# Spreading per-head rows over the partitions: 64-row matmuls or DMAs from a DRAM tile

## Chip, cores and metric

The kernel runs on one core of one Trainium2 chip. The metric is the device time of one execution in microseconds; 2156.14 us is the median of three runs before the change.

## The reference

A trunk of two layers over 512 tokens of width 1024, in float32. Each layer is a half-step SwiGLU FFN, a token mixer, and another half-step FFN; every sublayer has an RMSNorm before and after it and is modulated by shift, scale and gate vectors made from a conditioning vector. Layer 0's mixer is an mLSTM (4 heads), layer 1's a Mamba-2 SSD (32 heads in 4 groups). What matters here are the scalars per head and token:

```python
# mLSTM, per head; the kernel takes all 512 tokens as one chunk
b = cumsum(lf); log_d = b[t] - b[s] + ig[s]      # s <= t
m_t = max over s of log_d
s = (q @ k.T) * exp(log_d - m_t)
h = (s @ v) / max(|sum(s)|, exp(-m_t))
# Mamba-2, per head, chunks of 128 tokens
a = cumsum(dt * A)
y = ((C @ B.T) * exp(a[t] - a[s]) * dt[s]) @ x + exp(a[t]) * (C @ state)
```

In both, a matrix with the source token in the partitions needs a row over the target tokens (the running maximum, or `a`) in every partition.

## The kernel before

Features or tokens lie in the 128 partitions, 512 columns to a tile. All large products are made of float32r heads and rests: `mm3` (L175) issues three matmuls, head by head (L177), head by rest (L178) and rest by head (L179, by the order of the operands). Weights arrive in units of 128 x 1024 through `unit` (L150): a DMA on SP's queue into one of four `raw` buffers (L153), a copy to the head on ACT (L165), and the rest on DVE (L166), into one of three `wh` and `wl` buffers each. `proj` (L468) runs eight blocks of `mm3` over a unit into one of four `mm` PSUM banks; other PSUM work takes one of four `aux` banks (`ps_aux`).

SBUF working tiles come from 52 slots of 128 x 512 (`slot`, L98), handed on in the order in which they are freed. The program is written as a list of steps, in which `weave` (L1038) and `spread` (L1046) put projections between the steps of the mixers' heads; a scheduler then fixes the order of each engine's queue at build time, by readiness and the order of writing. At run time each queue is in order.

mLSTM: `rows` (L673) makes running sums and maxima for the heads as rows of [32, 512] tiles, and `split_rows` (L625) turns such a tile into a float32r [64, 512] tile, heads over rests (ACT L628, DVE L629). `pick(h)` (L632) is a stationary operand of 64 rows that selects row h and its rest; one matmul then spreads that row over 128 partitions. `head` (L713) does so for the negated maximum `nM` (L716), reads the result from PSUM on ACT (Relu L720, Exp L721), and for the denominator's `nm` (L748), with an exponential on ACT behind it (L750, `em`).

Mamba-2: `rows` (L803) makes `a` by a scan (L814) and splits it (L816). `ssm(g)` (L901) takes the eight heads of a group, two to a `yp` bank. For each head one matmul spreads `a` (L956); ACT makes the decay in `w` (four Relu L959, one Exp L961); DVE multiplies by the masked scores (L963); four matmuls L965 per head (the trace counts each as two) apply it. For each pair of heads a matmul with the operand `pair` (L948) puts one row into 64 partitions and the other into the other 64, for 384 columns (L970); ACT takes its exponential (`ea`, L972); DVE multiplies the state's share by it (L976) and adds it (L979).

The step of a Mamba pair, whose matmuls the change is about:

```python
                    pa = ps_aux()
                    matmul(pa, pick(h), self.ar[0:64], start=True, stop=True)
                    w = slot(name="w")
                    for c in range(4):
                        act(w[:, c * P:(c + 1) * P], pa[:, c * P:(c + 1) * P], AF.Relu, scale=-1.0,
                            bias=cols[:, P + c * 32 + h:P + c * 32 + h + 1])
```

The trunk weaves `ml.head(0..3)` with the value and output-gate projections (L1126 to L1129, with `pump`, which adds the modulation's steps L194 to L199), `mb.ssm(0..2)` with projections of the next group (L1151 to L1156), and spreads `mb.ssm(3)` over projections of `z` and the output product of groups 0 to 2 (L1157 to L1161).

Of the kernel before, what the change touches and what calls it, by code (L numbers as in the profile page):

```python
# [9 lines left out]
F32 = mybir.dt.float32  # L10
# [5 lines left out]
P = 128  # L16
T = 512
# [12 lines left out]
# log1p(e) = e * (c0 + e * (c1 + ...)) on [0, 1], relative error below 1e-8  # L30
# [26 lines left out]
def trunk(ctx: ExitStack, tc: tile.TileContext, i: dict, out: bass.AP):  # L57
# [21 lines left out]
    class Slots:  # L79
        """Tiles of one size, each place with a tag of its own; a place is handed on in the order of the frees."""  # L80
# [30 lines left out]
    # ------------------------------------------------------------ constants  # L111
# [29 lines left out]
    sel_f = const.tile([64, 32], F32, name="sel_f")  # L141
    nc.gpsimd.tensor_tensor(sel_f, ident[0:64, 0:32], ident[0:64, 32:64], ALU.add)
    sel = const.tile([64, 32], F32R, name="sel")
    nc.gpsimd.tensor_copy(sel, sel_f)
# [4 lines left out]
    # ------------------------------------------------------------ weights  # L149
    def unit(src, n=1024, hold=False, soon=True):  # L150
        """A block of weights [128, n] as its float32r head and the exact rest, in tiles of `step` columns."""
        raw = rawp.tile([P, 1024], F32, tag="raw", name="raw")
        nc.sync.dma_start(raw[:, :n], src)  # L153
        if hold:
            step = T
            his = [slot(F32R, "wh") for _ in range(-(-n // T))]
            los = [slot(F32R, "wl") for _ in range(-(-n // T))]
        else:
            step = 1024
            his = [whp.tile([P, 1024], F32R, tag="wh", name="wh")]  # L160
            los = [wlp.tile([P, 1024], F32R, tag="wl", name="wl")]
        with tc.high_priority() if soon else nullcontext():
            for q, (hi, lo) in enumerate(zip(his, los)):
                a, b = q * step, min(q * step + step, n)
                act(hi[:, :b - a], raw[:, a:b], AF.Copy)  # L165
                tt(lo[:, :b - a], raw[:, a:b], hi[:, :b - a].bitcast(F32), ALU.subtract)  # L166

        def part(a, w):
            q = a // step
            c = slice(a - q * step, a - q * step + w)  # L170
            return his[q][:, c], los[q][:, c]
        part.tiles = his + los if hold else []
        return part

    def mm3(ps, stat, mov, first, last):  # L175
        """ps += stat.T @ mov for operands given as (head, rest)."""
        matmul(ps, stat[0], mov[0], start=first, stop=False)  # L177
        matmul(ps, stat[0], mov[1], start=False, stop=False)  # L178
        matmul(ps, stat[1], mov[0], start=False, stop=last)  # L179
# [5 lines left out]
    # ------------------------------------------------------------ adaLN  # L185
# [3 lines left out]
    def ada_kind(l, s, kind):  # L189
# [43 lines left out]
        def gate_rows(parts):  # L233
            """The gate times the post norm's weight, the same row in every partition."""
            G[l, s] = []
            for c in range(2):
                rows = []
                for name in ("gate_b", "norm_post"):
                    rows.append(slot(name="row"))
                    nc.sync.dma_start(rows[-1], i[name][l * 3 + s:l * 3 + s + 1, c * T:(c + 1) * T].to_broadcast([P, T]))  # L240
                ps = ps_aux()
                for q, t in enumerate(parts[c]):
                    matmul(ps, ones_r, t, start=q == 0, stop=q == 1)
                g = slot(name="grow")
                tt(g, ps, rows[0], ALU.add)
                stt(g, g, 0.5 if s != 1 else 1.0, rows[1], ALU.mult, ALU.mult)
                G[l, s].append(g)
                free(*rows, *parts[c])
                done_ps(ps)
# [17 lines left out]
    # ------------------------------------------------------------ norms  # L267
    def newton(out, r0, v):
        """out = r0 * (1.5 + v * r0 * r0), v = -0.5 * (mean + eps)."""
# [4 lines left out]
    def ones_mm(ps, src):  # L274
        """ps = the sum over the partitions of src, on every partition."""
# [6 lines left out]
    def rstat(src, scale):  # L282
        """rsqrt(scale * (sum over partitions of src) + eps) on every partition, in src's place."""
# [10 lines left out]
    def rcol(ss, more=None):  # L294
        """rsqrt((ss + more) / D + eps), [128, 1]"""
# [23 lines left out]
    class Pre:  # L319
        """x's modulated norm, tokens in partitions, to hm, features in partitions."""  # L320
# [44 lines left out]
    def dot(raws, v):  # L365
        """The sum over kc of block kc of the raws times v[:, kc]."""
# [8 lines left out]
    def dot_end(acc, col):  # L375
        """mod0[:, col] = the sum over the partitions."""
# [6 lines left out]
    class Start(Pre):  # L383
        """The first sublayer's input: scaled first, with the shift put in later."""
# [49 lines left out]
    class Post:  # L434
        """Adds the sublayer's normed, gated output to x, a block of tokens at a time."""
# [31 lines left out]
    # ------------------------------------------------------------ projections  # L467
    def proj(ps, wt, hm, sl, m=P):  # L468
        """ps[:m, sl] = (1024 x m weights).T @ hm; wt: a unit of [128, 8 * m]."""
# [4 lines left out]
    def out_main(y, units, acts, first, last):  # L474
        """y[t] += acts[k][:, t].T @ weights, 2 k a unit"""
# [10 lines left out]
    def out_tail(ys, groups, first, done):  # L486
        """The same, block of tokens by block; groups: a list of (units, acts) for each of ys."""
# [15 lines left out]
    def out_proj(units, acts, tail, post):  # L503
        """units: [2, n / 2, 128, 1024]; the second half's last `tail` units go block by block of tokens."""
# [18 lines left out]
    class Ffn:  # L523
# [7 lines left out]
        def weights_kept(self, f):  # L531
            """The weights of f, loaded to slots that keep them."""
# [18 lines left out]
        def early(self, k, hm, ps):  # L551
            """Block k's share in the first columns, without the shift; ps: a pair for each f."""
# [9 lines left out]
        def late(self, f, q, kept):  # L562
            """The shift's share of columns f."""
# [49 lines left out]
    # ------------------------------------------------------------ rows: log1p(exp(-|x|))  # L613
# [11 lines left out]
    def split_rows(src):  # L625
        """[32, T] rows as a float32r [64, T]: heads over rests."""
        t = slot(F32R, "rows")
        act(t[0:32], src, AF.Copy)  # L628
        tt(t[32:64], src, t[0:32].bitcast(F32), ALU.subtract)  # L629
        return t  # L630

    def pick(h):  # L632
        """Stationary operand that spreads row h (and its rest) over the partitions."""
        return sel[:, h:h + 1].to_broadcast([64, P])

    # ------------------------------------------------------------ mLSTM
    class Mlstm:
# [35 lines left out]
        def rows(self):  # L673
# [14 lines left out]
            self.nM = split_rows(m)  # L688
            self.nm = split_rows(b)
# [23 lines left out]
        def head(self, h):  # L713
            k, q, vt = self.k[h], self.q[h], self.vt[h]
            pm = ps_aux()
            matmul(pm, pick(h), self.nM[0:64], start=True, stop=True)  # L716
# [8 lines left out]
            done_ps(pm)  # L725
# [21 lines left out]
            pn = ps_aux()  # L747
            matmul(pn, pick(h), self.nm[0:64], start=True, stop=True)  # L748
            em = slot(name="em")
            act(em, pn, AF.Exp)  # L750
            done_ps(pn)
# [37 lines left out]
    # ------------------------------------------------------------ Mamba-2  # L789
    class Mamba:  # L790
# [12 lines left out]
        def rows(self):  # L803
# [12 lines left out]
            self.ar = split_rows(a)  # L816
# [18 lines left out]
            done_ps(ps)  # L835
            free(self.dtr, ta, tw)
# [15 lines left out]
        def conv(self, ch, hm, ps=None):  # L852
            """silu(conv) of the 128 channels of block ch, [channel, token]."""
# [47 lines left out]
        def ssm(self, g):  # L901
# [20 lines left out]
            for c in range(4):  # L922
# [6 lines left out]
                if c < 3:  # L929
# [9 lines left out]
                    else:  # L939
# [6 lines left out]
            tp = slot(F32R, "pair")  # L946
            pair = tp[0:64]
            nc.vector.tensor_copy(pair.rearrange("p (h e) -> p h e", e=64),  # L948
                                  sel_f[:, g * 8:g * 8 + 8].unsqueeze(2).to_broadcast([64, 8, 64]))
            for j in range(4):  # L950
                yp = ps_aux()
                for e in range(2):
                    hh = 2 * j + e
                    h = g * 8 + hh
                    pa = ps_aux()
                    matmul(pa, pick(h), self.ar[0:64], start=True, stop=True)  # L956
                    w = slot(name="w")
                    for c in range(4):
                        act(w[:, c * P:(c + 1) * P], pa[:, c * P:(c + 1) * P], AF.Relu, scale=-1.0,  # L959
                            bias=cols[:, P + c * 32 + h:P + c * 32 + h + 1])  # L960
                    act(w, w, AF.Exp, scale=-1.0)  # L961
                    done_ps(pa)
# [6 lines left out]
                pa, yi = ps_aux(), ps_aux()  # L969
                matmul(pa[:, P:], pair[:, j * P:(j + 1) * P], self.ar[0:64, P:], start=True, stop=True)  # L970
                ea = slot(name="ea")
                act(ea[:, P:], pa[:, P:], AF.Exp)  # L972
# [7 lines left out]
                done_ps(pa, yi, yp)  # L980
                free(ea)
                yield
            free(gs, Cf, tp, *xdt, *state[1:])
# [18 lines left out]
        def wout(self, *gs):  # L1002
            """Adds the share of the groups gs to yacc."""
# [34 lines left out]
    def weave(main, *others):  # L1038
        """Traces main's steps with the others' spread between them."""
# [6 lines left out]
    def spread(main, n, rest, m):  # L1046
        """Traces main's n steps with m of rest's spread evenly between them."""
# [6 lines left out]
    # ------------------------------------------------------------ the trunk  # L1054
# [77 lines left out]
    free(ml.nM, ml.nm)  # L1132
# [29 lines left out]
    free(mb.ar, mb.cols)  # L1162
# [8 lines left out]
def _layout(inputs):  # L1171
# [5 lines left out]
    def stat(w, m=P):  # L1177
        """[K, M] -> [M / m, 128, (K / 128) * m]: blocks of m columns, contiguous per partition."""
# [6 lines left out]
    def mov(w):  # L1185
        """[K, 1024] -> [2, K / 256, 128, 2 * 512]: blocks of 256 rows and 512 columns."""
# [6 lines left out]
    def cols(a):  # L1193
        """[..., n * 128] -> [128, ... * n]"""
        return c(a.reshape(-1, P).T)
# [60 lines left out]
```

## Time and profile before

| | |
|---|---|
| median of three runs | 2156.14 us (2155.45 to 2156.46) |
| profiled execution, first to last instruction | 2154.5 us |
| PE busy | 2129.8 us (99%), 10742 matmuls |
| DVE, ACT, POOL busy | 1259.7, 862.0, 11.0 us |
| granted TensorE clock, mean | 0.998 |
| DMA | 272.84 MB, mean 127 GB/s |

Of the profiled execution the page gives the span alone; the median of the runs is 1.6 us longer than it. Durations of matmuls in the trace overlap, since they are pipelined: how much of PE's time a matmul takes is read from the starts of its neighbours. The mLSTM heads lie at about 459 to 600 us, the Mamba heads at about 1429 to 1720 us.

### The profile page before, as it was taken

The page shows a single profiled execution, that of the slowest core. Times are in us where ns is not written, and L with a number is a line of the kernel's source. Part 1 is how long each engine was busy: PE and PEld are TensorE (multiplying, and loading weights), DVE is VectorE, ACT ScalarE, POOL GpSimd, SP SyncE. Part 2 cuts the span into 40 slices and gives each one's busy share as a digit, 9 for nine tenths or more (in the row PEclk, how much of TensorE's full clock was granted, in tenths as well). Part 3 has the DMA queues.
Part 4 walks back from the last instruction along what each step waited for, and adds up shares of the span by engine and source line. Part 5 has one row for each costly group of instructions (what it writes and reads, how often), then busy time and mean ns, then how long its engine had stood idle before and what let it go on. Part 6 is the DMA issues. An engine that isn't in the chain of part 4 may idle for free.

```text
span 2154.5 us, 27065 instructions
## 1 busy us (share of the span) xinstructions
PE 2129.8 (99%) x10742; PEld 1769.0 (82%) x10742; DVE 1259.7 (58%) x1942; ACT 862.0 (40%) x1420; POOL 11.0 (1%) x35
## 2 busy tenths in 40 slices
PE   7999999999999999999999999999999999999998
PEld 5888888988789888889888888987777789888887
DVE  8976524758885775237574323877887756333323
ACT  5433323535562333236333223646555645222221
POOL 0000000000000000000000000000000000000000
PEclk9999999999999999999999999999999999999999
DMA  7666534143435776343574333221221132233331
GB/s 273 188 198 222 188 98 132 50 134 121 127 108 180 241 228 196 96 144 101 176 231 128 98 98 120 79 62 57 78 60 59 59 118 79 83 96 96 98 107 59
DMA packets 81535, 272.84 MB, mean 127 GB/s; under 512 B 10241, under 2 KB 10369, under 8 KB 81409
## 3 DMA queue, kind: packets, MB, share of 16 engines
q1 hardware_dynamic: 81408, 271.12, 39.7%
q8 instruction: 84, 1.38, 0.3%
q14 instruction: 43, 0.34, 0.1%
HBM read 268.99 MB, written 2.10 MB: 126 GB/s over the span
## 4 chain that ended last, share of the span: by engine, by line
PE 95%; DVE 2%; DMA 1%; ACT 1%; issue 0%; SPq 0%; DVEq 0%; ACTq 0%
PE mm L177 25%; PE mm L179 25%; PE mm L178 25%; PE aux L177 4%; PE aux L179 4%; PE aux L178 4%; PE aux L965 1%; PE aux L336 1%; PE aux L974 1%; PE aux L743 1%; PE aux L956 1%; PE aux L934 0%; DMA a<-in_ada 0%; PE aux L729 0%; DMA raw<-in_ada_w 0%
## 5 line engine op out<-in xcount | busy, mean ns | idle before, releaser
L177 PE MATMUL mm<-hm,wh 128*128 128x512 f32 (+1 forms) x2128 | 773.7, 366 | 2.7 <-ACT hm L350 1.3
L179 PE MATMUL mm<-hm,wl 128*128 128x512 f32 (+1 forms) x2128 | 770.6, 363 | 0.0
L178 PE MATMUL mm<-hm,wh 128*128 128x512 f32 (+1 forms) x2128 | 770.0, 363 | 0.0
L165 ACT ACTIVATE wh<-raw 128x1024 fp32r<-128x1024 f32 (+1 forms) x402 | 372.0, 941 | 764.3 <-PE mm L178 279.2
L166 DVE TENSOR_TENSOR wl<-raw,wh 128x1024 fp32r<-128x1024 f32 (+1 forms) x402 | 427.5, 1075 | 415.4 <-ACT wh L165 407.6
L177 PEld LDWEIGHTS mm<-hm,wh 128*128 128x128 f32 x2128 | 399.2, 188 | 69.5 <-issue 6.9
L179 PEld LDWEIGHTS mm<-hm,wl 128*128 128x128 f32 x2128 | 400.3, 188 | 63.0 <-issue 3.3
L178 PEld LDWEIGHTS mm<-hm,wh 128*128 128x128 f32 x2128 | 400.3, 188 | 62.5 <-issue 3.6
L199 DVE SCALAR_TENSOR_TENSOR acc<-raw,csil,acc 128x1024 f32<-128x1024 f32 x112 | 143.7, 1283 | 146.5 <-DMA raw<-in_ada_w 145.7
L589 DVE TENSOR_TENSOR s<-s,mm 128x512 f32<-128x512 f32 (+1 forms) x97 | 59.9, 618 | 134.0 <-PE mm L179 133.9
L177 PE MATMUL mm<-wh,gh 128*128 128x512 f32 x352 | 137.5, 391 | 0.0
L179 PE MATMUL mm<-wh,gl 128*128 128x512 f32 x352 | 137.0, 389 | 0.0
L178 PE MATMUL mm<-wl,gh 128*128 128x512 f32 x352 | 137.0, 389 | 0.0
L177 PE MATMUL aux<-wh,gh 128*128 128x512 f32 x352 | 136.9, 389 | 0.0
L178 PE MATMUL aux<-wl,gh 128*128 128x512 f32 x352 | 136.9, 389 | 0.0
L179 PE MATMUL aux<-wh,gl 128*128 128x512 f32 x352 | 136.9, 389 | 0.0
L182 ACT ACTIVATE gh<-s 128x512 fp32r<-128x512 f32 (+1 forms) x100 | 57.9, 580 | 130.3 <-DVE s L589 121.6
L179 PEld LDWEIGHTS mm<-wh,gl 128*128 128x128 f32 x352 | 66.1, 188 | 13.8
L179 PEld LDWEIGHTS aux<-wh,gl 128*128 128x128 f32 x352 | 66.1, 188 | 13.8
L178 PEld LDWEIGHTS aux<-wl,gh 128*128 128x128 f32 x352 | 66.1, 188 | 13.7
L177 PEld LDWEIGHTS aux<-wh,gh 128*128 128x128 f32 x352 | 66.1, 188 | 13.7
L178 PEld LDWEIGHTS mm<-wl,gh 128*128 128x128 f32 x352 | 66.1, 188 | 13.5
(276 smaller groups left out, 2188.7 us busy)
## 6 DMA issues: line engine op xcount, KB each, us to landing
raw<-in_w SPq DMA_DIRECT2D x258, 512.0 KB, 3.7
raw<-in_ada_w SPq DMA_DIRECT2D x128, 512.0 KB, 4.2
raw<-in_mb_wx SPq DMA_DIRECT2D x24, 512.0 KB, 3.6
a<-in_ada SPq DMA_DIRECT2D x32, 256.0 KB, 5.4
raw<-in_mb_wz SPq DMA_DIRECT2D x16, 512.0 KB, 3.6
raw<-in_mb_wout SPq DMA_DIRECT2D x16, 512.0 KB, 3.6
raw<-in_ml_wkq SPq DMA_DIRECT2D x8, 512.0 KB, 3.9
raw<-in_ml_wv SPq DMA_DIRECT2D x8, 512.0 KB, 3.6
```

Source lines behind the costliest of these rows:

```text
L165: act(hi[:, :b - a], raw[:, a:b], AF.Copy)
L166: tt(lo[:, :b - a], raw[:, a:b], hi[:, :b - a].bitcast(F32), ALU.subtract)
L177: matmul(ps, stat[0], mov[0], start=first, stop=False)
L178: matmul(ps, stat[0], mov[1], start=False, stop=False)
L179: matmul(ps, stat[1], mov[0], start=False, stop=last)
L182: act(dst_h, src, AF.Copy)
L199: stt(st["acc"], raw, csil[:, kc:kc + 1], st["acc"], ALU.mult, ALU.add)
L336: nc.tensor.transpose(self.pt[d // 2][:, o:o + P], scr[:, d * P:(d + 1) * P], ident)
L589: tt(s[:, a:b], s[:, a:b], p[1][:, a:b], ALU.mult)
L743: matmul(num[j][:, c * P:], vt[c // 2][:, o:o + P], st[c][:, c * P:], start=c == 0, stop=c == 3)
L956: matmul(pa, pick(h), self.ar[0:64], start=True, stop=True)
L965: matmul(yp[e * 64:(e + 1) * 64, c * P:(c + 1) * P], xdt[c][:, hh * 64:(hh + 1) * 64], w[:, c * P:(c + 1) * P], start=True, stop=True)
```

## The change

The rows are written to a DRAM tile once, and each head's row is loaded from there into all partitions. `split_rows`, `pick`, `sel`, `sel_f` and `pair` go, and with them the matmuls L716, L748, L956 and L970 and the PSUM banks they wrote. The exponentials of L750 and L972 are taken once on the rows, ahead of the write. ACT reads the spread rows from SBUF. Comments and docstrings go too, so that line numbers stay close.

```diff
+    class Rows:
+        def __init__(self, name, src):
+            n = src.shape[0]
+            self.got = {}
+            self.ap = tc.dram_tile([n, T], F32, name=name)
+            nc.sync.dma_start(self.ap, src)
+
+        def load(self, key):
+            if key in self.got:
+                return
+            t = slot(name="bc")
+            w = P // len(key)
+            for q, h in enumerate(key):
+                nc.sync.dma_start(t[q * w:(q + 1) * w], self.ap[h:h + 1, :].to_broadcast([w, T]))
+            self.got[key] = t
+
+        def take(self, key):
+            self.load(key)
+            return self.got.pop(key)
...
-            self.nM = split_rows(m)
-            self.nm = split_rows(b)
+            self.nM = Rows("ml_nM", m[0:4])
+            act(b, b, AF.Exp)
+            self.em = Rows("ml_em", b[0:4])
...
-            pm = ps_aux()
-            matmul(pm, pick(h), self.nM[0:64], start=True, stop=True)
+            pm = self.nM.take((h,))
...
-            done_ps(pm)
+            free(pm)
+            em = self.em.take((h,))
+            if h < 3:
+                self.nM.load((h + 1,))
...
-            pn = ps_aux()
-            matmul(pn, pick(h), self.nm[0:64], start=True, stop=True)
-            em = slot(name="em")
-            act(em, pn, AF.Exp)
-            done_ps(pn)
...
-            self.ar = split_rows(a)
+            self.ar = Rows("mb_a", a)
...
+            act(a, a, AF.Exp)
+            self.ea = Rows("mb_ea", a)
...
-            tp = slot(F32R, "pair")
-            pair = tp[0:64]
-            nc.vector.tensor_copy(pair.rearrange("p (h e) -> p h e", e=64),
-                                  sel_f[:, g * 8:g * 8 + 8].unsqueeze(2).to_broadcast([64, 8, 64]))
...
-                    pa = ps_aux()
-                    matmul(pa, pick(h), self.ar[0:64], start=True, stop=True)
+                    pa = self.ar.take((h,))
+                    if e == 0:
+                        self.ar.load((h + 1,))
+                        ea = self.ea.take((h, h + 1))
+                    elif h < 31:
+                        self.ar.load((h + 1,))
...
+                    free(pa)
                     act(w, w, AF.Exp, scale=-1.0)
-                    done_ps(pa)
...
-                pa, yi = ps_aux(), ps_aux()
-                matmul(pa[:, P:], pair[:, j * P:(j + 1) * P], self.ar[0:64, P:], start=True, stop=True)
-                ea = slot(name="ea")
-                act(ea[:, P:], pa[:, P:], AF.Exp)
+                yi = ps_aux()
```

## Rows read from the trace of the kernel before

**Rows 1.** The page, chain that ended last: shares of the span by engine.

```profile
PE 95%; DVE 2%; DMA 1%; ACT 1%; issue 0%; SPq 0%; DVEq 0%; ACTq 0%
```

**Rows 2.** Busy time by stretch: us, engines' busy time, PEclk, DMA share, GB/s.

```profile
0.00:80.00 80.00, 65.08 (x301) 52.92 (x302) 68.96 (x225) 44.20 (x70) 3.96 (x16) 1.00 0.66 225
...
1462.00:1530.00 68.00, 68.00 (x326) 49.47 (x325) 53.03 (x80) 42.11 (x87) 0.00 (x0) 1.00 0.18 56
...
1660.00:1720.00 60.00, 60.00 (x285) 44.04 (x284) 43.80 (x66) 35.04 (x69) 0.00 (x0) 1.00 0.19 54
```

**Rows 3.** PE in order of time around one L956: start, us, instruction.

```profile
1462.41 0.39 PE L178 MATMUL mm<-hm,wh 128*128 128x512 f32 x1
1462.64 0.39 PE L179 MATMUL mm<-hm,wl 128*128 128x512 f32 x1
1462.95 0.50 PE L956 MATMUL aux<-rows,sel 64*128 64x512 f32 x1
1463.38 0.50 PE L177 MATMUL mm<-hm,wh 128*128 128x512 f32 x1
1463.72 0.40 PE L178 MATMUL mm<-hm,wh 128*128 128x512 f32 x1
```

**Rows 4.** PE in order of time around one L970.

```profile
1478.72 0.40 PE L179 MATMUL mm<-hm,wl 128*128 128x512 f32 x1
1479.05 0.44 PE L970 MATMUL aux<-rows,pair 64*128 64x384 f32 x1
1479.42 0.50 PE L177 MATMUL mm<-hm,wh 128*128 128x512 f32 x1
1479.75 0.39 PE L178 MATMUL mm<-hm,wh 128*128 128x512 f32 x1
```

**Rows 5.** PE in order of time around two L956 in a row.

```profile
1639.80 0.40 PE L178 MATMUL mm<-hm,wh 128*128 128x512 f32 x1
1640.13 0.72 PE L956 MATMUL aux<-rows,sel 64*128 64x512 f32 x2
1640.78 0.50 PE L179 MATMUL mm<-hm,wl 128*128 128x512 f32 x1
1641.12 0.40 PE L177 MATMUL mm<-hm,wh 128*128 128x512 f32 x1
```

**Rows 6.** The four lines' matmuls: ns min/median/max, first and last start in us.

```profile
L956 PE MATMUL aux<-rows,sel x32: 387/497/502, 1463.0 to 1698.4; 64*128 64x512 f32 x32
...
L970 PE MATMUL aux<-rows,pair x16: 328/442/443, 1470.6 to 1701.0; 64*128 64x384 f32 x16
...
L716 PE MATMUL aux<-rows,sel x4: 497/497/498, 458.9 to 553.4; 64*128 64x512 f32 x4
...
L748 PE MATMUL aux<-rows,sel x4: 497/497/497, 478.4 to 573.5; 64*128 64x512 f32 x4
```

**Rows 7.** DMA issues: count, KB each, median us to landing.

```profile
row<-in_gate_b SPq DMA_DIRECT2D x12, 256.0 KB, 4.2
...
out_x<-x SPq DMA_DIRECT2D x8, 256.0 KB, 2.1
```

**Rows 8.** The tile `row`: its loads (a broadcast row of 512) on SP's queue.

```profile
L240 SPq DMA_DIRECT2D row<-in_gate_b x12: 327/328/425, 79.9 to 1100.8; - x12
...
DMA to landing us min/median/max: 3.4/4.6/6.3
```

**Rows 9.** Line L628, ACT: ns min/median/max, first and last start in us.

```profile
L628 ACT ACTIVATE rows<-fg x1: 630/630/630, 431.0 to 431.0; 32x512 fp32r<-32x512 f32 x1
...
L628 ACT ACTIVATE rows<-a x1: 632/632/632, 1403.1 to 1403.1; 32x512 fp32r<-32x512 f32 x1
```

**Rows 10.** Waits (us, times, longest): whole span; 1425 to 1720; SP 1380 to 1720.

```profile
DVE acc L199 <- DMA raw<-in_ada_w: 145.7, 64, 4.6
...
ACT wh L165 <- PE mm L178: 37.1, 28, 4.7
...
SPq L153 <- DVE wl L166: 323.9, 39, 21.1
```

More of the change, by code (lines that the diff above doesn't have):

```diff
@@ L140, in trunk @@
                             pattern=[[0, 4], [1, P]], channel_multiplier=-1)
[L141 to L144, printed above, removed]
     csil = const.tile([P, ND], F32, name="csil")
@@ L623, in softplus_tail @@
         return ta
[L625 to L634, printed above, removed]
+    class Rows:
[15 more added lines that the diff above has]
+            return self.got.pop(key)
     class Mlstm:
@@ L979, in ssm @@
                 tt(y[:, P:], y[:, P:], ea[:, P:], ALU.add)
-                done_ps(pa, yi, yp)
+                done_ps(yi, yp)
                 free(ea)
                 yield
-            free(gs, Cf, tp, *xdt, *state[1:])
+            free(gs, Cf, *xdt, *state[1:])
         def gated(self, g):
@@ L1131, in trunk @@
         ml.gate(h)
-    free(ml.nM, ml.nm)
     post = Post(0, 1, (0, 2))
@@ L1161, in trunk @@
         pass
-    free(mb.ar, mb.cols)
+    free(mb.cols)
     post = Post(1, 1, (1, 2), mb.yacc)
```

## The prediction

> **What bounds the kernel now.** I read the chain of waits first: followed back from the last instruction, 95% of the span is TensorE work and 1% is DMA [rows 1]. So an instruction taken off PE's queue is worth its place in that queue, as long as nothing else becomes late. The table by stretch [rows 2] says whether something would. In the Mamba mixer (1462 to 1720 us) PE is busy in 68.00 of 68.00 us and in 60.00 of 60.00, DVE in 53.03 and 43.80 of them, ACT in 42.11 and 35.04, at a granted clock of 1.00; the DMA engines are busy 0.18 and 0.19 of the time, at 56 and 54 GB/s. The views by line of the four matmuls that go [rows 6] give counts, lengths and places: 32 of L956, 16 of L970, 4 of L716, 4 of L748. Their length of 497 ns (442 for the 384-column one) is not their price, because lengths of neighbours overlap; the price is read from the starts.
>
> **Price of a removed matmul.** Around an L956 [rows 3], two neighbours of the 128-row stream start 0.23 us apart (1462.41, 1462.64). With L956 between, the second start behind 1462.64 comes at 1463.72: 1.08 us in place of 2 x 0.23, so 0.62 us for one 64-row matmul. It costs 0.08 before it starts, 0.43 until the next starts, and 0.11 behind that. For L970 [rows 4] it is 1479.75 - 1478.72 - 0.46 = 0.57. Two L956 in a row [rows 5] share the change of shape: 1641.12 - 1639.80 - 0.46 = 0.86 for both. The PE timeline has four such pairs, and once an L956 with an L970 behind it, which I read in the same way at 0.79 for the two. The sum:
>
> - 23 single L956 x 0.62 = 14.3
> - 4 pairs of L956 x 0.86 = 3.4
> - the mixed pair = 0.8
> - 15 single L970 x 0.57 = 8.6
> - 4 L716 and 4 L748, single, x 0.62 = 5.0 (their 497 ns is L956's [rows 6])
>
> Together 32.1 us. Bounds: counting only the time until the next start (0.43, and 0.37 for L970) gives 40 x 0.43 + 16 x 0.37 = 23; the single price for all 56 gives 40 x 0.62 + 16 x 0.57 = 34.
>
> A rule of the Trainium skill would make this far smaller: TensorE: Matmul & The Clock Gate, section "Why this matters for your kernels", says that a matmul over few rows takes the time of one over 128. It is a rival below; the rows speak against it (1.08 us where the stream with one matmul more would take 0.69).
>
> **What else goes.** ACT loses 16 exponentials of L972, four of L750 and three splits; DVE loses three splits and four copies of `pair`; PSUM loses one bank per head. ACT and DVE have room [rows 2], so I cost this at nothing either way. What covers it is PE's full queue.
>
> **What comes: the row tiles.** There are two writes of [4, 512] and two of [32, 512], and two exponentials of a row tile on ACT, about 0.63 us each by the L628 rows [rows 9]. Each load waits on SP's queue until its write has landed; the nearest rows are the output's writes, 2.1 us [rows 7]. The rows before are ready at about 431 and 1403 us [rows 9], and first used at 458.9 and 1463.0 [rows 6]: 28 and 60 us for about 2 + 5 us of write and load. Cost nothing. What is queued behind a waiting load on SP are weight loads. SP already stands still before weight loads for 323.9 us of 340, up to 21.1 us at once [rows 10], because all four `raw` buffers are full; a weight that comes a few us later is still there in time, and no wait of `wh` on a DMA is among the longest of that stretch, where ACT waits for PE to free `wh` (37.1 us) [rows 10]. Cover gone, each write would cost at most its 2.1 us and the first load its 5: some 10 us.
>
> **What comes: the loads.** Four for `nM`, four for `em`, 32 for `ar` (128 partitions, 256 KB each), and 32 half loads for `ea`: 72 DMAs, 76 with the writes. SP's time is 76 x 0.33 = 25 us [rows 8], inside its standing still. Bytes: 48 x 256 KB = 12.6 MB over the 240 us of the Mamba heads, 52 GB/s more on 55; in the first 80 us the same engines moved 225 GB/s at 0.66 busy [rows 2]. So no bound from bandwidth. Latency: the nearest row is the load that spreads a gate row over 128 partitions, the same shape, landing after 3.4 to 6.3 us, median 4.6 [rows 8].
>
> Now the one term that matters. ACT's L959 of head h waits for that load, and behind it on ACT stand the weight split L165, the convolution's L859 and the next head. The code asks for head h+1 when head h is taken. In the timeline, 15 of the 31 gaps between neighbouring heads are longer than 4.6 us, and there the load is hidden. In 16 it isn't, if it starts no earlier than the head before: the shortfalls of 4.6 less the gap add to 42 us (the pair of [rows 5] has one of 4.3). That is one end; the other is nothing, or a gain of a few us from the freed PSUM banks (PE's waits for the head's chain are short already, so 3 us at most). I take 3 us of loss, near the low end, for three reasons. A load's only conditions are its slot and its row, and neither is tied to the head before. In these places PE has projections that wait for no head. And the nearest row for a late DMA is L199, where DVE waits for `raw` 64 times, 145.7 us in all and 4.6 at most [rows 10], while PE stays full.
>
> **Sum.** 32.1 - 3 = 29 us off the profiled execution, whose span of 2154.5 us lies 1.6 under the median of 2156.14; what lies around the span doesn't change. 2156.1 - 29 = 2127 us. A difference under 0.2% (4.3 us) can't be told from none here.
>
> **Rivals.**
>
> 1. *Late loads (slower).* At the close heads, ACT waits for `bc` in place of PE; the weighted tile comes late, and PE's queue, which runs in order, stands at L965. For it: half of the gaps are shorter than a landing, the last group's heads come close together from 1679 us on, and a slot freed shortly before is what the load gets. Against it: other work for PE, and the places where a load can be issued earlier. Place: the Mamba heads. Price: 42 - 32 = 10 us over, 2166. It decides from 2.0 us per close head on (32 / 16). The Trainium skill, DMA: Bandwidth & Descriptors, "Anatomy of one DMA", has the wait of a DMA on the issuing sequencer, ahead of its dispatch; SP's waits agree (323.9 us, [rows 10]).
> 2. *Half hidden.* The same, but PE fills half of the shortfalls: 32 - 21 = 11 us gained, 2145, with a spread of 2136 to 2156.
> 3. *The matmul was cheap.* If a 64-row matmul cost only its share of the stream, 40 x 0.23 + 16 x 0.17 = 12 us go and the time is 2144. The rule cited above would have this; [rows 3 to 5] speak against it.
>
> That the change doesn't do what it says is no rival: the matmuls leave the program, and no equal is put in.
>
> **How the numbers follow.** Forecast 0.62, rival 1 0.12, rival 2 0.21, rival 3 0.05. Faster by over 0.2% (under 2151.8): 0.62 + 0.05 + 0.15 of rival 2 = 0.82. Within: the other 0.06 of rival 2. Slower: 0.12. The likeliest gives 2127. The range begins at 2118 (34 us gone, 3 gained from the banks, and 1 us for a different order) and ends at 2152, so that rival 1 and the slow end of rival 2 are outside.
>
> **What would show it.** Right: no PE line of 64 rows; the Mamba stretch some 24 us and the mLSTM stretch some 5 us shorter; PE still full; the starts of the 128-row stream 0.23 us apart through a head; loads of `bc` landing in 4 to 5 us. Wrong: PE idle at L965 or at L743 behind a DVE or ACT that waited for `bc` or `em`; ACT's L959 with tens of us of waits for a DMA and a PE that isn't full; weight splits that wait for `raw`; a granted clock under 1.00.

## The result, and the profile after

The changed kernel takes 2124.03 us (median of four runs, 2123.18 to 2125.51) beside 2156.3 us of the kernel before on the same chip: a ratio of 0.9851 with a 95% interval of 0.9837 to 0.9864, 32.3 us less. Forecast were 2127 us, in a range of 2118 to 2152. The profiled execution has a span of 2122.3 us, 32.2 less than before.

Busy time by stretch in the Mamba mixer after the change (us, busy time of PE, PEld, DVE, ACT and POOL, granted clock, DMA share, GB/s), against [rows 2]; PEld is TensorE's loading of weights:

```profile
1462.00:1530.00 68.00, 68.00 (x360) 54.53 (x359) 58.61 (x87) 38.06 (x67) 0.00 (x0) 1.00 0.36 114
...
1600.00:1660.00 60.00, 58.83 (x310) 46.88 (x309) 50.14 (x75) 37.80 (x76) 0.00 (x0) 1.00 0.35 110
```

The kernel before has in the second of these stretches:

```profile
1600.00:1660.00 60.00, 60.00 (x290) 44.06 (x289) 45.69 (x68) 33.69 (x70) 0.00 (x0) 1.00 0.20 62
```

PE is all but as full as before (58.83 of 60 us in the second stretch), and it gets more done: 360 matmuls in the same 68 us in place of 326, at the same granted clock of 1.00, the upper of its two levels (2.4 GHz). DVE's share went up (58.61 us in place of 53.03) because its work is nearly the same (1254.9 us in all, 1259.7 before) and the stage is shorter. The DMA engines move 114 GB/s in place of 56. The chain of waits, followed back from the end, holds PE almost alone; this time it could be followed for a fifth of the span only (PE 20%, every other engine 0%), so it isn't the view to read here. The page's busy times over the whole span are:

```profile
PE 2095.6 (99%) x10686; PEld 1760.5 (83%) x10686; DVE 1254.9 (59%) x1935; ACT 861.3 (41%) x1401; POOL 11.3 (1%) x33
```

PE's busy time fell by 34.2 us (from 2129.8), and its idle time rose by 2.0 (from 24.7 to 26.7 us).

The PE timeline around heads whose decay matrices are applied (after the change) answers to [rows 3 to 5]:

```profile
1471.71 0.39 PE L174 MATMUL mm<-hm,wh 128*128 128x512 f32 x1
1471.94 0.40 PE L175 MATMUL mm<-hm,wl 128*128 128x512 f32 x1
1472.17 0.40 PE L173 MATMUL mm<-hm,wh 128*128 128x512 f32 x1
1472.41 0.39 PE L174 MATMUL mm<-hm,wh 128*128 128x512 f32 x1
1472.72 1.58 PE L972 MATMUL aux<-w,xdt 128*64 128x128 f32 x16
1474.23 0.50 PE L175 MATMUL mm<-hm,wl 128*128 128x512 f32 x1
```

The stream runs 0.23 us from start to start and nothing with 64 rows stands in it. What is left is the other change of shape, to the 64 columns of L972 (L965 before): 0.31 us before it, and 1.51 for sixteen records. In the Mamba stretch the trace before has 43 stays of PE in the 64-row shape (matmuls of that shape with none of another between) and 31 in the 64-column shape; after the change it has none and 26.

The loads, in the list of DMA issues after the change (count, KB each, median us to landing):

```profile
bc<-mb_a SPq DMA_DIRECT2D x32, 256.0 KB, 3.4
...
bc<-mb_ea SPq DMA_DIRECT2D x32, 128.0 KB, 3.2
...
bc<-ml_nM SPq DMA_DIRECT2D x4, 256.0 KB, 4.2
bc<-ml_em SPq DMA_DIRECT2D x4, 256.0 KB, 4.6
...
mb_a<-a SPq DMA_DIRECT2D x1, 64.0 KB, 1.6
mb_ea<-a SPq DMA_DIRECT2D x1, 64.0 KB, 2.8
```

In the mLSTM mixer a row lands as late as [rows 8] had it; in the Mamba mixer it lands in 3.4 us. Who waits for them, in the waits of 1400 to 1690 us (us, times, longest), and the queue of SP from 1380 to 1690:

```profile
ACT w L966 <- DMA bc<-mb_a: 4.9, 3, 2.4
...
DVE wl L162 <- DMA bc<-mb_a: 2.0, 1, 2.0
```

```profile
SPq L149 <- DVE wl L162: 148.0, 36, 15.0
SPq L636 <- PE aux L972: 15.5, 7, 4.6
```

ACT stands three times for a row, 4.9 us in all. DVE stands once until a row's load has landed, at L162, which doesn't read the row; why is not settled here. PE itself has no wait for a tile made from a row; its weight loads have five of up to 0.4 us, 1.8 us in all. SP's standing still before weight loads fell from 323.9 us in 340 [rows 10] to 148.0 in 310: some 105 us are now spent standing before the loads of L636, most of them, by what ends these waits, until a slot is free.

ACT's first instruction on a row shows how early the heads can start. The first line is the view of the line L966 after the change, the second that of L959 before (min/median/max ns, first and last start):

```profile
L966 ACT ACTIVATE w<-bc,cols x128: 385/388/404, 1410.3 to 1672.4; 128x128 f32<-128x128 f32 x128
```

```profile
L959 ACT ACTIVATE w<-aux,cols x128: 346/368/425, 1464.5 to 1700.9; 128x128 f32<-128x128 f32 x128
```

The heads' work on ACT begins 54 us earlier, some 12 us behind the scan that makes `a`: it needs neither a turn on PE nor a PSUM bank any more. In the first two groups ACT starts a head 9 to 54 us before PE's first L972 of that head; in the last group the lead is 4 to 6 us for seven heads of eight, no longer than before the change (3.4 to 7.3 us). One instruction takes 20 ns more when it reads SBUF.

### The profile page after: what moved, and what is told of

The parts are those of the page before. It is cut to its first block, busy times and chain, and to the rows that moved or that the text cites. A ratio compares the mean times of both kernels' runs of the same rounds, so it can differ in the third digit from the quotient of the medians.

```text
span 2122.3 us, 27083 instructions
## 1 busy us (share of the span) xinstructions
PE 2095.6 (99%) x10686; PEld 1760.5 (83%) x10686; DVE 1254.9 (59%) x1935; ACT 861.3 (41%) x1401; POOL 11.3 (1%) x33
## 5 line engine op out<-in xcount | busy, mean ns | idle before, releaser
L162 DVE TENSOR_TENSOR wl<-raw,wh 128x1024 fp32r<-128x1024 f32 (+1 forms) x402 | 427.2, 1075 | 401.4 <-ACT wh L161 390.8
```

## Experiments

The theory: the gain is the time that PE lost around the 64-row matmuls, most of it for the change of its shape; the loads are hidden. Rivals: the gain came from PSUM banks or from a shorter chain of the heads; the loads are hidden only by being asked for one head ahead, or just barely. All ratios below are to the kernel before, run beside the kernel in question.

**1. The same matmuls over 128 rows.**

```diff
-    sel_f = const.tile([64, 32], F32, name="sel_f")
+    sel_f = const.tile([P, 32], F32, name="sel_f")
...
         tt(t[32:64], src, t[0:32].bitcast(F32), ALU.subtract)
+        ts(t[64:P], mask[64:P], 0.0, None, ALU.mult)
...
-            matmul(pm, pick(h), self.nM[0:64], start=True, stop=True)
+            matmul(pm, pick(h), self.nM, start=True, stop=True)
```

> The kernel before with the spreading matmuls kept, but over 128 rows (the rows' tile and the selectors are filled up with zeros), so that PE never leaves its 128-row shape for them. Theory (the price is the change of shape): each keeps only its place in the stream, 0.23 us (0.17 for 384 columns) in place of 0.62 (0.57): 31 singles x 0.39 + 4 pairs x 0.40 + 0.4 + 15 x 0.40 = 20 us less, about 2136. Rival A (the number of rows doesn't matter, the gain of the change came from PSUM banks or from the heads' chain): about 2156, no change.

Measured: 2139.98 us, ratio 0.9927 (0.9912 to 0.9942), 15.6 us less. The PE timeline of this kernel shows the places. In the stream, L957 (L956 before) now takes what any matmul takes:

```profile
1459.96 0.39 PE L179 MATMUL mm<-hm,wl 128*128 128x512 f32 x1
1460.19 0.40 PE L957 MATMUL aux<-rows,sel 128*128 128x512 f32 x1
1460.43 0.39 PE L177 MATMUL mm<-hm,wh 128*128 128x512 f32 x1
1460.65 0.40 PE L178 MATMUL mm<-hm,wh 128*128 128x512 f32 x1
...
1476.77 1.09 PE L966 MATMUL aux<-w,xdt 128*64 128x128 f32 x8
1477.79 0.50 PE L957 MATMUL aux<-rows,sel 128*128 128x512 f32 x1
1478.22 1.09 PE L966 MATMUL aux<-w,xdt 128*64 128x128 f32 x8
```

0.24 us to the next start in place of 0.43, and no loss on either side. The 20 us expected lie outside the interval (12.5 to 19.0 us). The last three lines show a part of the shortfall: beside a 64-column matmul there is a change of shape in any case, and there L957 still takes 0.43. The trace has two such places between 64-column matmuls and four behind some. By the page PE's busy time fell by 18.2 us (2129.8 to 2111.6); the rest of the shortfall is not explained. Rival A falls as a cause of the whole: the same banks and the same chain are there, and half of the change's gain comes from the shape alone.

**2 and 3. One mixer at a time.** The changed kernel with the Mamba class of the kernel before (cut below), and with its mLSTM class.

```diff
-                    pa = self.ar.take((h,))
...
+                    pa = ps_aux()
+                    matmul(pa, pick(h), self.ar[0:64], start=True, stop=True)
```

> The change in the mLSTM mixer alone; Mamba keeps its matmuls. Theory: 8 x 0.62 = 5 us less, 2151. Rival B (the loads cost about what the matmuls did; all of the gain is from elsewhere): 2156.

> The change in the Mamba mixer alone; mLSTM keeps its matmuls. Theory: 27 us less, 2129; this and the mLSTM-only kernel add to the whole. Rival A would have more than 27 here, since the two or three PSUM banks per pair of heads come free here.

Measured: mLSTM alone 2151.13 us, ratio 0.9981 (0.9971 to 0.9990), 4.5 us less; Mamba alone 2128.24 us, ratio 0.9872 (0.9857 to 0.9887), 27.4 us less. Together 31.9 of the 32.3. The prediction's sum has 5.0 and 27.1.

**4. The loads with the matmuls beside them.**

```diff
+    def dummy(n=T):
+        pd = ps_aux()
+        matmul(pd[:, :n], ones_r[0:64], ones_r[0:64].unsqueeze(1).to_broadcast([64, n // P, P]), start=True, stop=True)
+        done_ps(pd)
...
+                    dummy()
                     pa = self.ar.take((h,))
```

> The changed kernel with the 56 matmuls over 64 rows put back at their places, on ones, into a PSUM bank that nobody reads: the loads still carry the data. Theory: PE's time comes back and the loads cost nothing, so 2124 + 32 = 2156, within 4 us of the kernel before. Rival A (the gain was that ACT no longer waits for a PSUM result): stays near 2124, below 2140. Rival C (the loads cost some us that hide in the gain): above 2160.

Measured: 2151.49 us, ratio 0.9978 (0.9968 to 0.9987): 4.1 us under the kernel before (2.8 to 6.9), at the edge of what the theory allowed, and far from both rivals. So the matmuls bring back 27 of the 32 us without carrying any data, and the 72 loads and their waits leave little to see: PE is idle for 25.9 us of the profiled execution, beside 24.7 in the kernel before. The 4 us are in PE's busy time, 5.0 us less by the page (2124.8 beside 2129.8). The tiles `w` are often ready ahead here, and the scheduler puts L980 (L965 before) right behind the 64-row matmul:

```profile
1469.96 0.39 PE L180 MATMUL mm<-hm,wl 128*128 128x512 f32 x1
1470.28 0.50 PE L144 MATMUL aux<-ones_r 64*128 64x512 f32 x1
1470.71 1.09 PE L980 MATMUL aux<-w,xdt 128*64 128x128 f32 x8
```

There, one change of shape serves both and the matmul adds 0.43 us, not 0.62. 22 stays in the 64-row shape border on 64-column matmuls in this way, where the kernel before has 6: 16 x 0.19 = 3 us. That this and 29 stays in the 64-column shape in place of 31 are the whole of it is argued, not tested.

**5. Nothing asked for ahead.**

```diff
-            if h < 3:
-                self.nM.load((h + 1,))
...
                     if e == 0:
-                        self.ar.load((h + 1,))
                         ea = self.ea.take((h, h + 1))
-                    elif h < 31:
-                        self.ar.load((h + 1,))
```

> The changed kernel without the lines that ask for the next head's row: each row is asked for where it is taken. Theory: a load's conditions are its slot and its row alone, not its place in the list of steps, so within 3 us of the changed kernel, 2124. Rival D (asking one head ahead is what hides the loads): the 36 loads of nM and ar show, between 16 x 2 and 36 x 3 us: 2156 or more.

Measured: 2122.58 us, ratio 0.9853 (0.9836 to 0.9869), as the changed kernel. Rival D falls, but not in the way that the theory has it: the step's place in the list does move the load. The eighth Mamba head's load and ACT's first instruction on its row, first in the changed kernel, then here:

```profile
1445.80 0.48 SPq L636 DMA_DIRECT2D bc<-mb_a  x1
...
1459.76 1.26 ACT L966 ACTIVATE w<-bc,cols 128x128 f32<-128x128 f32 x4
```

```profile
1451.99 0.33 SPq L636 DMA_DIRECT2D bc<-mb_a  x1
...
1455.09 1.29 ACT L961 ACTIVATE w<-bc,cols 128x128 f32<-128x128 f32 x4 [2.46 <-DMA bc<-mb_a]
```

Over the 32 heads the median time from a load's issue to that first instruction is 14.3 us in the changed kernel and 5.6 us here. There, 28 of 31 loads leave before ACT starts on the head before; here, 16 do. ACT waits 11.1 us for rows in place of 4.9, and the kernel's time is the same.

**6 and 7. The late-loads rival made true.** `ar`'s rows get two buffers of their own, or one, in place of slots (and the rest one slot fewer; the kernel with two also keeps its ones in one tile fewer, for space). With one buffer, the rows are asked for where they are taken. The cut is of the kernel with two.

```diff
+    ownp = pool("ownp", 2)
...
-            t = slot(name="bc")
+            if self.pool:
+                t = self.pool.tile([P, T], F32, tag="own", name="bo")
+            else:
+                t = slot(name="bc")
```

> The changed kernel with two buffers of their own for the rows of ar (one slot fewer for the rest): a head's load can't start before the head two earlier has been read by ACT, which is the condition of the late-loads rival. If that rival's mechanism is there, close heads run at the pace of a landing (3.4 us) and PE stands at the weighted tiles' matmuls: up to 20 us, 2124 + 20 = 2144. Theory with PE's other work as cover: within 4 us, 2124 to 2128.

> One buffer for the rows of ar, asked for where it is taken (one slot fewer for the rest): each load starts when ACT has read the row before, so no load is hidden behind a head. Late-loads rival: a head can't be shorter than landing plus four Relu, 3.4 + 1.2 = 4.6 us; the shortfalls of the 16 close heads, 42 us, show: 2166. Theory with PE's other work as cover: part of it, under 15 us, below 2139.

Measured: two buffers 2125.64 us, ratio 0.9865 (0.9851 to 0.9880), an interval that overlaps the changed kernel's (0.9834 to 0.9863, experiment 11); one buffer 2129.89 us, ratio 0.9883 (0.9868 to 0.9897), clear of it: 2155.33 x (0.9883 - 0.9849) = 7 us slower. In the trace of the kernel with one buffer, no load leaves before ACT starts on the head before, and ACT's heads start no closer than 4.4 us apart. So with no load hidden behind the head before, 7 us show, where the prediction had 42 us of shortfall. The waits of this kernel (us, times, longest), ACT's for the row and PE's for the tile made from it:

```profile
ACT w L968 <- DMA bo<-mb_a: 26.2, 16, 3.5
```

```profile
PE aux L973 <- DVE w L971: 2.2, 2, 1.2
```

ACT waits 26.2 us in place of 4.9, sixteen times, but only 2.2 us of it reach PE as a wait. Both of PE's waits are at heads of the last group, at the two shortest leads of ACT over PE, 2.7 and 3.2 us; the first head's lead is 51 us here too. Of the rest, a part is that PE goes to the 64-column shape 29 times in place of 26. That the cover is ACT's lead and PE's other work fits this, but neither was taken away alone.

**8. Every load twice.**

```diff
-                nc.sync.dma_start(t[q * w:(q + 1) * w], self.ap[h:h + 1, :].to_broadcast([w, T]))
+                for _ in range(2):
+                    nc.sync.dma_start(t[q * w:(q + 1) * w], self.ap[h:h + 1, :].to_broadcast([w, T]))
```

> The changed kernel with every spreading load issued twice, the second behind the first into the same tile: bytes doubled (14.7 MB more) and the row is there some 6 to 7 us after the issue in place of 3.4. Theory: slots are free early enough for most, so under 6 us, 2124 to 2130. Late-loads rival (the margin is small): 20 us or more, 2144.

Measured: 2131.13 us, ratio 0.9890 (0.9875 to 0.9905), 9 us slower than the changed kernel: over the theory's 6 and well under the rival's 20. Neither expected where it goes. The scan that makes `a` starts at 1403.2 us in place of 1397.5, so 5.7 us of it are lost ahead of the Mamba heads; PE's longest wait after the first 100 us is one in the mLSTM mixer (first line), and the timeline of DVE shows what stood before it:

```profile
PE mm L174 <- DVE wl L162: 4.9, 1, 4.9
```

```profile
458.89 1.28 DVE L195 SCALAR_TENSOR_TENSOR acc<-raw,csil,acc 128x1024 f32<-128x1024 f32 x1 [2.66 <-DMA raw<-in_ada_w]
463.89 1.28 DVE L195 SCALAR_TENSOR_TENSOR acc<-raw,csil,acc 128x1024 f32<-128x1024 f32 x1 [3.71 <-DMA raw<-in_ada_w]
465.10 2.35 DVE L162 TENSOR_TENSOR wl<-raw,wh 128x1024 fp32r<-128x1024 f32 x2
```

```profile
SPq L637 <- DMA bc<-ml_em: 11.6, 4, 6.3
```

The second load of a row stands on SP until the first has landed, 11.6 us in this stage (last line). Behind it are the loads of the modulation's weights: the pair of them that SP issues from 445.23 us on in the changed kernel starts at 448.96 here. DVE waits for such a load in its queue (3.71 us), and the rest of a projection's weight, L162, stands behind DVE's wait. So at PE's longest wait a load held on SP costs time by way of a weight that is late, not by way of a head that is late. The other 2 to 3 us are lost from there on: in the Mamba mixer SP stands 53.8 us for first loads of `ar`, and PE's waits come to 3.1 us in place of 1.5.

**9 to 12. The other change of shape.** If a change of shape has a price, the one to 64 columns has it too. The two heads of a pair are applied together, first one behind the other and then in turns; the changed kernel itself ran beside them; and last the same pairing was put into the kernel before. The cut is of the kernel in turns.

```diff
+                    ws.append(w)
+                    if e:
+                        for c in range(4):
+                            for f in range(2):
+                                hf = 2 * j + f
+                                matmul(yp[f * 64:(f + 1) * 64, c * P:(c + 1) * P], xdt[c][:, hf * 64:(hf + 1) * 64],
+                                       ws[f][:, c * P:(c + 1) * P], start=True, stop=True)
+                        free(*ws)
```

> The changed kernel with the weighted tiles of a pair of heads applied together, first head, then second (L972 of both behind the second head's tile). Theory (a change of PE's shape has a price of its own): the stream now changes to the 64-column shape 16 times in place of 26; two runs of 8 records stand 2 x 1.02 us to the next start, one of 16 1.51, so 10 x 0.53 = 5 us less than the changed kernel, about 2119. Rival (the price was a wait, not the shape): 2124, no change, or slower if the second tile is late.

> The same, with the matmuls of the two heads in turns, so that neighbours go to the two halves of the columns. If neighbours in different column halves run beside each other, each of 16 runs falls from 1.51 to about 0.9 us: 10 us less than the sequential one, 2109. If the array works on one at a time: as the sequential one, 2119.

> The changed kernel itself, beside the other two on the same chip: 2124 by the first measurement, ratio 0.985.

> The kernel before, with its 64-row matmuls, and the two heads of a pair applied together in turns as in the previous experiment. Theory (the pairing is worth its shape changes and the overlap of column halves, whatever brings the rows): about 12 us less, 2143. Rival (the pairing needs weighted tiles that are ready ahead, which only the changed kernel has): under 5 us, above 2150.

Measured: one behind the other 2120.11 us, ratio 0.9835 (0.9818 to 0.9851); in turns 2110.88 us, ratio 0.9792 (0.9777 to 0.9807); the changed kernel 2123.07 us, ratio 0.9849 (0.9834 to 0.9863); pairing in the kernel before 2146.67 us, ratio 0.9963 (0.9949 to 0.9978). The sequential pairing gains 3 us where 5 were expected, and its interval meets the changed kernel's: 21 stays in the 64-column shape are left in the trace, not 16, eleven of sixteen records and ten of eight, since other matmuls still come between. In turns is clear. The PE timelines of the sequential kernel and of the one in turns:

```profile
1473.17 0.40 PE L174 MATMUL mm<-hm,wh 128*128 128x512 f32 x1
1473.50 1.58 PE L977 MATMUL aux<-w,xdt 128*64 128x128 f32 x16
1475.01 0.94 PE L983 MATMUL aux<-cv,state 128*128 128x128 f32 x6
```

```profile
1508.22 1.09 PE L977 MATMUL aux<-w,xdt 128*64 128x128 f32 x16
```

In turns, sixteen records take 1.02 us to the next start (1509.25) in place of 1.51. Eleven pairs stand like this, 11 x 0.49 = 5.4 us. The other five stand as eight and eight records in the sequential kernel (2 x 1.02 us) and as fourteen and two in the one in turns (1.02 and 0.36 us), 5 x 0.66 = 3.3. Together that is 8.7 of the 9.2 us between the two kernels. In the kernel before the pairing is worth 8.5 us (4.7 to 11.0), half-way between the theory's 12 and the rival's 5, so neither comes out as it stood. All sixteen pairs stand there as fourteen and two records; what parts them was not tested. The kernel in turns, 2110.88 us, beats both kernels of this study by 12 and 44 us.

## Why the prediction was right

**The price of a removed matmul** held. 32.1 us from the starts of neighbours stood against 32.3 measured, 5.0 and 27.1 by mixer against 4.5 and 27.4. That the first two agree to 0.2 us is luck in part. PE's busy time fell by 34.2 us, more than the sum: PE goes to the 64-column shape 26 times in place of 31, and from their first start to the next other start these stays take 29.5 us in place of 32.1. PE's idle time rose by 2.0 us. Neither is in the 32.1, and the two nearly cancel. The sum also leaves out that six of its places border on 64-column matmuls, where [rows 3 to 5] don't give the price. Experiment 1 shows that the price above the stream's 0.23 is the change of shape: over 128 rows the same matmul takes 0.24 us to the next start, not 0.43, and loses nothing around it. The Trainium skill, TensorEngine Tiling (Array Packing), section "Key Properties", says that changing the tiling mode drains the engine; 0.62 against 0.23 us agrees, though no row shows a drain as such. By the rule of the Trainium skill that the prediction cites (TensorE: Matmul & The Clock Gate, "Why this matters for your kernels") 12 us would have gone; the rule speaks of the matmul by itself, and the runs decide for the stream around it. Rival 3 is out.

**The loads as cover** held, and more widely than the prediction had it. Its 3 us for late loads was a choice near the low end of a range, and it is the one term that was mis-sized. PE's idle time rose by 2.0 us in the profiled execution and by 0.6 in that of experiment 11 (25.3 us), and no wait of PE in the Mamba mixer names a tile made from a row. The other end of the range, 42 us, stood under the condition that a load starts no earlier than the head before. That condition doesn't hold: 28 of 31 loads start earlier. The heads themselves are still close: on ACT, 12 of 31 gaps are shorter than 4.6 us, and they fall short by 24 us in all. With 16 of 31 starting earlier (experiment 5) nothing is lost, with none (experiment 7) 7 us. So asking one head ahead moves the loads, but the kernel's time doesn't hang on it. The low end that the prediction chose was right, as far as the runs show, for the first two reasons that it gave, a load that isn't tied to the head before and PE's other work; the lead of the first heads on ACT, which start 54 us before the old ones, is a third that it didn't have. What held the heads back in the kernel before, PE's order or the banks, was not tried alone.

**Late loads (rival 1) and half hidden (rival 2)** don't come about, even where experiment 7 gives the rival its condition on the loads (the first heads still run far ahead on ACT). Where experiment 8 held loads back, PE's longest wait was not at the rival's place either: it was for a weight behind them on SP's queue and on DVE's, in the mLSTM mixer. The prediction had costed SP's queue at nothing, with the four `raw` buffers as cover; that is right for 76 DMAs, and not for twice as many loads with waits between them.

**Smaller terms.** Bandwidth: 58 GB/s more in 1462 to 1530 us and 48 in 1600 to 1660, where 52 were worked out. Landing: 3.4 us where 4.6 was taken, 4.2 to 4.6 in the mLSTM mixer. Writes: 1.6 and 2.8 us in the Mamba mixer, with 2.1 taken. DVE and ACT, costed at nothing, didn't become the bound: DVE is at 58.61 of 68 us.

## What to carry to other kernels

Read a small matmul's price on a full TensorE from the starts of its neighbours: one of another shape costs the change into it and out of it, here 0.62 us where the engine's stream has 0.23 per matmul. Moved to DMA, the same work raised PE's idle time by 2 us at most here, and in experiments 5 to 7 time was clearly lost (7 us) only when no load left before ACT started on the head before. Count how many leave before that; then look at what stands behind the loads in the issuing queue, not only at who reads the tile. Where the change of shape can't be avoided, put the matmuls of one shape together, and those of different column halves in turns: here that gave another 12 us. And when a sum meets the measured time to a fraction of a us, compare busy and idle time before and after, to see whether errors cancel.

## What was not expected

The prediction has no word on the 64-column matmuls that stay. Alternating between the two halves of the columns, they overlap: 1.02 us for sixteen records in place of 1.51 in the same shape and count (experiments 9 and 10). The Trainium skill, TensorEngine Tiling (Array Packing), "Key Properties", says that different tiles can load weights and multiply in parallel, and the run agrees; that eight records of one half also take 1.02 us (1476.77 to 1477.79 in experiment 1) means that the second head's matmuls cost next to nothing there.
